# Routing stage of a mixture-of-experts block re-ordered: three tiles gathered within the last tile's logits

## Chip, cores and metric

The kernel runs on one core of one Trainium2 chip. The metric is the device time of one execution in microseconds (us); lower is better. TensorE is PE (its weight loads PEld), VectorE is DVE, ScalarE is ACT, GpSimd is POOL, and SyncE is SP, which here only issues transfers.

## What is computed

One decoder block for 512 tokens of width 1024, in float32: a token mixer (retention heads and gated DeltaNet heads, one input and one output projection), then a mixture of 16 experts in 4 groups of 4. Only the second half matters here:

```python
h = h + gate_m * mixer(xm)                       # ends in the output projection
xf = rms_norm(h) * (1 + scale_f) + shift_f
group = top_1(softmax(xf @ w_group + b_group))   # one of 4 groups
experts = top_2(softmax((xf @ w_router)[group] + b_router))
for each token and each of its two experts e:
    y = (silu(xf @ w_gate[e]) * (xf @ w_up[e])) @ w_down[e]
    out += combine_weight * y
out = rms_norm(h + gate_f * out)
```

## The kernel before

Tokens are handled in four tiles of 128 rows, t = 0 to 3; L is 3, the last. The order of the instructions on each engine is the order in which the code emits them; a framework adds the waits. Every engine works through its own list strictly in order.

**Output projection and routing (lines 1140 to 1376).** For each tile PE makes the output projection in four column blocks q (tile `py`). `stats` makes the new residual `hb` and the scaled rows `xf` on DVE, half a tile at a time, and sums squares on ACT. `scales` turns them into 1/rms (`rs`) with 13 tiny DVE instructions. `turn` transposes half of xf on PE (`xrt`), ACT copies it out (`xrT`), and PE multiplies it with the router's weights (`lg`, `logits`). `xf_rows` scales xf by rs on ACT, adds the row `Brow` and writes the rows to DRAM (`xfd`). `routes` picks group and experts on DVE and leaves a 0/1 mask `M` (token by expert); it runs once for tiles 0 to 2 and once for tile 3. Products of M with triangular and all-one matrices on PE (`pos`) give each token's place in its expert's list. `places` copies them to `posa` and makes the selection matrices `sel01` for experts 0 and 1. `slots` computes addresses, and POOL scatters the token numbers to a list in DRAM, `il`, with two small indirect transfers for each tile. `pick` gathers the rows of experts 0 and 1 by matmuls of xf with sel01 into four PSUM banks `pse` (`xe` in the trace), accumulated over the four tiles.

**Weight parts.** Every weight block of 1 MB is loaded into a raw buffer and split into a high part `hi` (ACT cast, line 293) and a low part `lo` (DVE subtraction, line 294), each in two halves of 128x1024; a product needs three passes of PE. A block is called (expert, j): j = 0 to 3 for gate and up, 4 and 5 for down. `split_next` splits the next one in the order (0,0) to (0,3), (1,0) to (1,3), (0,4), (0,5), (2,0) to (2,3), (1,4), (1,5) and so on. There are six hi/lo pairs and up to eight raw buffers. SP issues the loads in the same order, each one when its raw buffer is free.

**Experts.** For each expert e PE runs `gate_up` (48 matmuls `gu`); after each block j, `after` releases the block's parts and calls split_next for j < 3. DVE multiplies silu(gate) by up (`hh`), PE transposes hh (`xe<-sq,hh`), and `down` (`py`) of expert e runs inside the step of expert e+1. Experts 0 and 1 take their rows from pse (`x_first`: `th`, `tl` for expert 0, `x` for expert 1). From expert 2 on the rows are gathered from xfd by an indirect transfer (`x_load`, tile X) with token numbers `toks`. These come from the list il: POOL loads it (`ilr`), DVE casts it (`ilf`), PE transposes it (`il`) and DVE makes rows and toks (`slot_rows`, called after block (0,0)). `more_blocks` (DVE, called after block (1,0)) plans extra blocks for experts with over 128 tokens; they are worked off inside expert 5's step.

Of the kernel before, what the change touches and what calls it, by code (L numbers as in the profile page):

```python
# [114 lines left out]
def body(ctx, tc, x, c, mod_w, mod_b, norm_mix_w, w_in, gdn_conv_w, gdn_a_log, gdn_dt_bias, gdn_norm_w, w_out,  # L115
# [171 lines left out]
    def split(key, ks=(0, 2048), n=256, n0=256, eng=None):  # L287

        if key not in parts:
            parts[key] = (hi_free.pop(0), lo_free.pop(0))  # L290
        r = loaded[key]
        hi, lo, rw = (flat(t, n)[:, ks[0] // n:ks[1] // n, :n0] for t in (*parts[key], r))
        act.copy(out=hi, in_=rw)  # L293
        (eng or dve).tensor_tensor(out=lo, in0=rw, in1=hi.bitcast(F32), op=ALU.subtract)  # L294
        if ks[1] == 2048:
            free_raw(key)
# [648 lines left out]
    def xT_half(src, half, evac):  # L945

        pt = pst("xrt")
# [238 lines left out]

    def xf_rows(t):
        act.activation(out=xf[t], in_=xf[t], func=AF.Copy, scale=rs[:, t:t + 1])
        pool.tensor_tensor(out=xf[t], in0=xf[t], in1=Brow, op=ALU.add)
        pool.dma_start(out=xfd[t * P:(t + 1) * P], in_=xf[t])  # L1190
# [65 lines left out]
    def places(t0, n):  # L1256

        T = slice(t0, t0 + n)
        dve.tensor_copy(out=posa[:, T], in_=ppos[:, t0 * NE:(t0 + n) * NE].rearrange("p (t e) -> p t e", e=NE))
        for t in range(t0, t0 + n):  # L1260
            for e in range(2):
                dve.tensor_scalar(out=sel01[:, t, e], in0=iota, scalar1=posa[:, t, e:e + 1], scalar2=M[:, t, e:e + 1],
                                  op0=ALU.is_equal, op1=ALU.mult)
# [33 lines left out]
    def turn(t, half, first_):  # L1297

        if first_:
            xts[t] = xT_half(xf[t], half, act.copy)  # L1300
        else:
            logits(pl[:, t * 20:(t + 1) * 20], xts[t], half, True)

    for t in range(NT):
        py = [pst("py") for _ in range(2)]
        for q in range(4):
            w2 = two(("o", q), 256)
            for k in range(KB):
                for i, (a, w) in enumerate(PASSES):
                    pe.matmul(py[q // 2][:, (q % 2) * 256:(q % 2 + 1) * 256], lhsT=mhl[t][a][:, k], rhs=w2[w][:, k],  # L1310
                              start=(k == 0 and i == 0), stop=(k == KB - 1 and i == 2))
                if k == 3 and t and q < 2:
                    turn(t - 1, q, False)
                if k == 3 and q == 2 and t == L:
                    split_next(1, None, pool)
# [9 lines left out]
            if q == 0 and t:  # L1325
                turn(t - 1, 1, True)
            if q == 1:
                if t == L:
                    split_next(1, None, pool)
# [5 lines left out]
                if t:  # L1335
                    xf_rows(t - 1)
            if q == 3:
# [6 lines left out]
    turn(L, 0, False)  # L1344
    turn(L, 1, True)
# [5 lines left out]
    turn(L, 1, False)  # L1351
    places(0, L)
    slots(0, L)
    xf_rows(L)
    pse = [pst("xe") for _ in range(4)]

    def pick(t0, n):

        for t in range(t0, t0 + n):
            for k in range(KB):  # L1360
                pe.matmul(pse[k // 2][:, (k % 2) * 256:(k % 2 + 1) * 256], lhsT=xf[t][:, k * P:(k + 1) * P],
                          rhs=sel01[:, t].rearrange("p e q -> p (e q)"), start=(t == 0 and k % 2 == 0),
                          stop=(t == NT - 1), skip_group_check=True)

    pick(0, L)
    w3 = routes(L, 1)
    for o, l in ((ppos[:, L * NE:NT * NE], stri), (pcn, ones)):
        pe.matmul(o, lhsT=l, rhs=M[:, L], start=False, stop=True, skip_group_check=True)
    places(L, 1)
    cnt = cp.tile([P, NE], F32, name="cnt")  # L1370
    dve.tensor_copy(out=cnt, in_=pcn)
    pick(L, 1)
    slots(L, 1)
    split_next()
# [7 lines left out]
    pool.dma_start(out=ilr, in_=il.rearrange("(r q) o -> r (q o)", q=P))  # L1382
# [267 lines left out]
    for e in range(NE):  # L1650
# [3 lines left out]
        def after(j, e=e):  # L1654
# [143 lines left out]
```

## Time and profile before

| | |
|---|---|
| device time, median of 3 runs | 1088.85 us (1085.78 to 1088.94) |
| the profiled execution | 1089.13 us, its span 1087.3 us |
| PE busy | 963.2 us, 89% of the span |
| DVE busy | 736.0 us, 68% |
| ACT busy | 518.0 us, 48% |
| POOL busy | 295.7 us, 27% |
| DMA | 217.91 MB, mean 200 GB/s |

The span runs from the first to the last instruction of the core; the device time has 1.83 us around it. Busy times of the engines overlap, so they don't add up to the span. All times below count from the start of the span. A line such as `655.32 12.44 PE L1361 MATMUL xe<-sel,xf ... x48 [3.18 <-DVE sel L1262]` reads: 48 instructions of line 1361 began at 655.32 us and took 12.44 us together; PE sat idle 3.18 us before them, until DVE had written sel. The trace counts a float32 matmul twice.

### The profile page before, as it was taken

To read this page: it belongs to the slowest core of one execution; us is meant where nothing else is said; L and a number is where in the kernel's file an instruction comes from. 1 tells how busy PE (TensorE), PEld (TensorE's weight loads), DVE (VectorE), ACT (ScalarE), POOL (GpSimd) and SP (SyncE) were. 2 spreads that over 40 slices of the span, in tenths; PEclk is the share of its full clock that TensorE was granted. 3 is DMA by queue.
4 is the path that set the end of the run, shared out by engine and by line. 5 is a ranking of instruction groups with operands and counts; after the bars stand their busy time and mean duration, and the time that the engine had idled before them with its cause. 6 is when DMAs were issued, how large, how long until landed. Compare 5 with 4: busy or idle time off the path is not lost. (4 is left out here: it accounts for less than half of the span.)

```text
span 1087.3 us, 14839 instructions
## 1 busy us (share of the span) xinstructions
PE 963.2 (89%) x5672; PEld 835.7 (77%) x5672; DVE 736.0 (68%) x1167; ACT 518.0 (48%) x750; POOL 295.7 (27%) x281
## 2 busy tenths in 40 slices
PE   4899989989889999999999977599967899999972
PEld 2579957768799999999989975478846688888851
DVE  3478246767886652566448594699766789898966
ACT  4453134433342331362233333478655778888823
POOL 2018733553447645000000154111100111111103
PEclk8999998989989989999999988799988999999987
DMA  9857742232345532232157245789784799999941
GB/s 297 268 177 249 222 138 83 83 113 82 128 136 145 165 117 79 69 107 79 40 161 252 98 154 75 283 322 388 245 307 171 287 389 384 376 383 365 358 164 78
DMA packets 139538, 217.91 MB, mean 200 GB/s; under 512 B 14942, under 2 KB 72830, under 8 KB 138692
## 3 DMA queue, kind: packets, MB, share of 16 engines
q1 hardware_dynamic: 124640, 182.45, 48.9%
q0 software_dynamic: 11296, 30.66, 9.1%
q10 hardware_dynamic: 3524, 3.78, 1.0%
q8 instruction: 47, 0.77, 0.3%
q14 instruction: 31, 0.25, 0.1%
HBM read 204.98 MB, written 21.16 MB: 208 GB/s over the span
## 5 line engine op out<-in xcount | busy, mean ns | idle before, releaser
L294 DVE TENSOR_TENSOR lo<-raw,hi 128x1024 fp32r<-128x1024 f32 (+1 forms) x194 | 242.0, 1287 | 57.9 <-ACT hi L293 57.8
L293 ACT CAST hi<-raw 128x1024 fp32r<-128x1024 f32 (+1 forms) x198 | 197.4, 1043 | 28.1 <-PE gu L1492 21.6
L1064 PE MATMUL pm<-lo,xh 128*128 128x256 f32 x640 | 186.5, 291 | 11.5 <-DVE ty L650 7.1
L1064 PE MATMUL pm<-hi,xh 128*128 128x256 f32 x640 | 186.5, 291 | 0.0
L1064 PE MATMUL pm<-hi,xl 128*128 128x256 f32 x640 | 185.9, 290 | 0.0
L1064 PEld LDWEIGHTS pm<-lo,xh 128*128 128x128 f32 x640 | 125.8, 196 | 12.4 <-issue 7.2
L1064 PEld LDWEIGHTS pm<-hi,xh 128*128 128x128 f32 x640 | 125.9, 197 | 0.5
L1064 PEld LDWEIGHTS pm<-hi,xl 128*128 128x128 f32 x640 | 125.8, 197 | 0.3
L1492 PE MATMUL gu<-lo,xth 128*128 128x512 f32 x256 | 103.7, 405 | 10.7 <-DVE lo L1559 9.2
L1492 PE MATMUL gu<-hi,xtl 128*128 128x512 f32 x256 | 103.1, 403 | 2.0 <-DVE xtl L1460 2.0
L1492 PE MATMUL gu<-hi,xth 128*128 128x512 f32 x256 | 103.1, 403 | 0.0
L393 POOL TENSOR_TENSOR rawm<-rawm 128x512 f32<-128x512 f32 (+2 forms) x96 | 100.3, 1044 | 7.7
L493 POOL DMA_DIRECT2D rawm<-in_mod_w_dram x32 | 29.7, 927 | 213.8 <-PE modp L510 202.3
L1064 PE MATMUL pm<-xl,hi 128*128 128x512 f32 x168 | 70.1, 417 | 2.0 <-ACT hi L293 1.6
L1064 PE MATMUL pm<-xh,lo 128*128 128x512 f32 x168 | 71.1, 423 | 0.5 <-DVE lo L294 0.5
L1064 PE MATMUL pm<-xh,hi 128*128 128x512 f32 x168 | 70.9, 422 | 0.0
L1492 PEld LDWEIGHTS gu<-lo,xth 128*128 128x128 f32 x256 | 49.4, 193 | 23.4 <-DVE lo L1559 9.6
L1008 ACT ACTIVATE sg<-pm 128x512 f32<-128x512 f32 x32 | 18.9, 597 | 95.9 <-PE pm L1064 81.1
L1514 PE MATMUL py<-lo,th 128*128 128x512 f32 x144 | 61.8, 429 | 1.4 <-ACT th L1505 1.4
L391 POOL TENSOR_TENSOR rawm<-rawm,cs 128x1024 f32<-128x1024 f32 x32 | 61.4, 1918 | 0.6
L1451 POOL DMA_INDIRECT X<-xfd,toks x14 | 20.3, 1448 | 148.8 <-PE xe L1472 128.8
L1492 PEld LDWEIGHTS gu<-hi,xtl 128*128 128x128 f32 x256 | 49.2, 192 | 14.3 <-DVE xtl L1460 2.4
(405 smaller groups left out, 2037.0 us busy)
## 6 DMA issues: line engine op xcount, KB each, us to landing
raw<-in_w_in_dram SPq DMA_DIRECT2D x32, 1024.0 KB
raw<-in_w_up_dram SPq DMA_DIRECT2D x26, 1024.0 KB
raw<-in_w_gate_dram SPq DMA_DIRECT2D x24, 1024.0 KB
raw<-in_w_down_dram SPq DMA_DIRECT2D x20, 1024.0 KB
rawm<-in_mod_w_dram POOLq DMA_DIRECT2D x32, 512.0 KB, 5.2
rawe<-in_w_down_dram SPq DMA_DIRECT2D x9, 1024.0 KB
rawe<-in_w_up_dram SPq DMA_DIRECT2D x8, 1024.0 KB
mod<-in_mod_w_dram SPq DMA_DIRECT2D x7, 1024.0 KB
```

Source lines behind the costliest of these rows:

```text
L293: act.copy(out=hi, in_=rw)
L294: (eng or dve).tensor_tensor(out=lo, in0=rw, in1=hi.bitcast(F32), op=ALU.subtract)
L391: pool.tensor_tensor(out=r, in0=r, in1=cs.unsqueeze(2).to_broadcast([P, KB, n]), op=ALU.mult)
L393: pool.tensor_tensor(out=r[:, :m], in0=r[:, :m], in1=r[:, m:2 * m], op=ALU.add)
L493: pool.dma_start(out=r, in_=mw[:, :, (16 + i) * P:(17 + i) * P])
L1008: act.activation(out=sg, in_=pt, func=AF.Sigmoid)
L1064: pe.matmul(o, lhsT=l, rhs=r, start=st, stop=sp__)
L1451: pool.indirect_dma_start(out=X, out_offset=None, in_=xfd, in_offset=bass.IndirectOffsetOnAxis(ap=at, axis=0), bounds_check=S - 1, oob_is_ ...
L1492: pe.matmul(pt, lhsT=xx[a][k // 4][:, k % 4], rhs=hi_lo[w][:, k % 4], start=(k == 0 and i == 0), stop=(k == KB - 1 and i == 2))
L1514: pe.matmul(pt, lhsT=tt[a][:, k], rhs=hi_lo[w][:, k], start=(k == 0 and i == 0), stop=(k == 3 and i == 2))
```

## The change

In tile 3's step: the low parts of blocks (0,1) and (0,2), which POOL made, are left to DVE and made after the gather; ACT still makes the high parts there. Brow is added by DVE for tiles 2 and 3, and earlier for tiles 0 to 2. The gather (`pick`) of tiles 0 to 2 is interleaved with tile 3's transposes and logits. The list of slots is loaded after the memsets of X, and cast and transposed after block (1,0) instead of (0,0); more_blocks moves to after block (2,0). A split of a block that stood ahead of the experts stands within them.

```diff
-    def split(key, ks=(0, 2048), n=256, n0=256, eng=None):
+    def split(key, ks=(0, 2048), n=256, n0=256, eng=None, what="hl"):
...
-        act.copy(out=hi, in_=rw)
+        if "h" in what:
+            act.copy(out=hi, in_=rw)
+        if "l" not in what:
+            return
         (eng or dve).tensor_tensor(out=lo, in0=rw, in1=hi.bitcast(F32), op=ALU.subtract)
...
+    def xf_scale(t):
+        act.activation(out=xf[t], in_=xf[t], func=AF.Copy, scale=rs[:, t:t + 1])
+
     def xf_rows(t):
-        act.activation(out=xf[t], in_=xf[t], func=AF.Copy, scale=rs[:, t:t + 1])
-        pool.tensor_tensor(out=xf[t], in0=xf[t], in1=Brow, op=ALU.add)
+        (pool if t < L - 1 else dve).tensor_tensor(out=xf[t], in0=xf[t], in1=Brow, op=ALU.add)
         pool.dma_start(out=xfd[t * P:(t + 1) * P], in_=xf[t])
...
+    def split_upper():
+
+        key = order[nsplit[0] + len(held_back)]
+        for h in (0, 1):
+            split(key, (h * 1024, h * 1024 + 1024), 512, 512, what="h")
+        held_back.append(key)
+
     def split_next(n=1, half=None, eng=None):
         for _ in range(n):
+            if held_back:
+                key = held_back.pop(0)
+                for h in (0, 1):
+                    split(key, (h * 1024, h * 1024 + 1024), 512, 512, what="l")
+                nsplit[0] += 1
+                continue
...
             if q == 0 and t:
                 turn(t - 1, 1, True)
+                xf_scale(t - 1)
+                xf_rows(t - 1)
             if q == 1:
                 if t == L:
-                    split_next(1, None, pool)
+                    split_upper()
                     w012 = routes(0, L)
...
-                if t:
-                    xf_rows(t - 1)
-            if q == 3:
+            if q == 3 and t < L:
                 turn(t, 0, True)
...
-    turn(L, 0, False)
-    turn(L, 1, True)
     pe.matmul(ppos[:, :L * NE], lhsT=stri, rhs=M[:, :L].rearrange("p t e -> p (t e)"), start=True, stop=False,
...
+    turn(L, 0, True)
+    places(0, L)
+    selections(0)
+    stats(L, 1, py[1])
+    selections(1)
+    selections(2)
+    slots(0, L)
+    scales(L, 1)
+    pse = [pst("xe") for _ in range(4)]
...
+    pick(0)
+    turn(L, 0, False)
+    turn(L, 1, True)
+    pick(1, range(4))
     turn(L, 1, False)
-    places(0, L)
-    slots(0, L)
-    xf_rows(L)
...
-    pick(0, L)
+    xf_scale(L)
     w3 = routes(L, 1)
+    pick(1, range(4, KB))
+    pick(2)
     for o, l in ((ppos[:, L * NE:NT * NE], stri), (pcn, ones)):
         pe.matmul(o, lhsT=l, rhs=M[:, L], start=False, stop=True, skip_group_check=True)
+    xf_rows(L)
     places(L, 1)
+    selections(L)
...
-    pick(L, 1)
+    pick(L)
     slots(L, 1)
-    split_next()
...
-    pool.dma_start(out=ilr, in_=il.rearrange("(r q) o -> r (q o)", q=P))
...
     def slot_rows():
 
+        dve.tensor_copy(out=ilf, in_=ilr)
         pt = ps_m.tile([P, 512], F32, tag="m", name="il")
...
     for t in (X, X2):
         pool.memset(t, 0.0)
+    pool.dma_start(out=ilr, in_=il.rearrange("(r q) o -> r (q o)", q=P))
...
-            if e == 0 and j == 0:
+            if e == 1 and j == 0:
                 slot_rows()
                 x_load(toks[:, 8:9], X)
-            if e == 1 and j == 0:
+            if e == 2 and j == 0:
                 more_blocks()
...
         if e == 0:
+            split_next()
             xx1 = x_first(1)
-            split_next(2)
+            split_next(4)
```

On PE, from tile 3's transposes (`xrt`) and logits (`lg`) to the last gather (`xe`), the list of before reads as follows (`sel_5062` is sel01, `pos` the list products):

```order
L950 MATMUL xrt<-sq_94,xf_5055 128x128 x4
L957 MATMUL lg<-wr,xrT 128x20 x4
L950 MATMUL xrt<-sq_94,xf_5055 128x128 x4
L1346 MATMUL pos<-M,sq_94 128x48
L1348 MATMUL pos<-Mc,ones 128x48
L1350 MATMUL pos<-Mc,ones 128x16
L957 MATMUL lg<-wr,xrT 128x20 x4
L1361 MATMUL xe<-sel_5062,xf_5054 128x256 x16
L1361 MATMUL xe<-sel_5062,xf_5055 128x256 x8
L1368 MATMUL pos<-M,sq_94 128x16
L1368 MATMUL pos<-M,ones 128x16
L1361 MATMUL xe<-sel_5062,xf_5055 128x256 x8
```

In the change the three list products of tiles 0 to 2 come first, and the last of them heads this piece of PE's list:

```order
L1369 MATMUL pos<-Mc,ones 128x16
L953 MATMUL xrt<-sq_94,xf_5055 128x128 x4
L1383 MATMUL xe<-sel_5062,xf_5054 128x256 x8
L960 MATMUL lg<-wr,xrT 128x20 x4
L953 MATMUL xrt<-sq_94,xf_5055 128x128 x4
L1383 MATMUL xe<-sel_5062,xf_5054 128x256 x4
L960 MATMUL lg<-wr,xrT 128x20 x4
L1383 MATMUL xe<-sel_5062,xf_5054 128x256 x4
L1383 MATMUL xe<-sel_5062,xf_5055 128x256 x8
L1397 MATMUL pos<-M,sq_94 128x16
L1397 MATMUL pos<-M,ones 128x16
L1383 MATMUL xe<-sel_5062,xf_5055 128x256 x8
```

The gather of tiles 0 to 2 has moved from behind the logits to between and behind them; the number of matmuls is the same.

On DVE, from the end of the gather to expert 0's `hh`, before (raw_4776 holds block (1,0), raw_88 (1,1), raw_5037 (1,2), raw_89 (1,3), raw_4775 at the end (0,4)):

```order
L1460 TENSOR_TENSOR tl<-xe,th 128x256 x4
L1593 CAST ilf<-ilr 64x128
L1460 TENSOR_TENSOR x_5912<-xe,x_5912 128x256 x4
L294 TENSOR_TENSOR lo_5036<-raw_4776,hi_5035 128x1024 x2
L294 TENSOR_TENSOR lo_5901<-raw_88,hi_5900 128x1024 x2
L294 TENSOR_TENSOR lo_5460<-raw_5037,hi_5459 128x1024 x2
L1396 CAST rows<-il 128x64
L1397 COPY rowsf<-il 128x64
L1401 TENSOR_SCALAR toks<-rows 128x64
L294 TENSOR_TENSOR lo_93<-raw_89,hi_92 128x1024 x2
L294 TENSOR_TENSOR lo_91<-raw_4775,hi_90 128x1024 x2
L1498 TENSOR_TENSOR hh<-hh,gu_5885 128x512
```

The same place on DVE with the change (blocks (0,1), then (0,2), (0,3), (1,0), (1,1), (1,2), (1,3), (0,4)):

```order
L1490 TENSOR_TENSOR tl<-xe,th 128x256 x4
L297 TENSOR_TENSOR lo_93<-raw_5037,hi_92 128x1024 x2
L1490 TENSOR_TENSOR x_5903<-xe,x_5903 128x256 x4
L297 TENSOR_TENSOR lo_91<-raw_89,hi_90 128x1024 x2
L297 TENSOR_TENSOR lo_5034<-raw_4775,hi_5033 128x1024 x2
L297 TENSOR_TENSOR lo_5036<-raw_4776,hi_5035 128x1024 x2
L297 TENSOR_TENSOR lo_5893<-raw_88,hi_5892 128x1024 x2
L297 TENSOR_TENSOR lo_5463<-rawe_5894,hi_5462 128x1024 x2
L297 TENSOR_TENSOR lo_93<-rawe_5895,hi_92 128x1024 x2
L297 TENSOR_TENSOR lo_91<-raw_5037,hi_90 128x1024 x2
L1528 TENSOR_TENSOR hh<-hh,gu_5873 128x512
```

Three blocks more stand between the gather and hh, and the cast of the list is gone. It stands in expert 1's part of DVE's list now, behind the subtraction of block (2,0), which takes the pair that block (1,0) frees:

```order
L1528 TENSOR_TENSOR hh<-hh,gu_5873 128x512
L297 TENSOR_TENSOR lo_5034<-raw_89,hi_5033 128x1024 x2
L1536 TENSOR_TENSOR tl<-xe,th 128x512
L297 TENSOR_TENSOR lo_5036<-raw_4775,hi_5035 128x1024 x2
L1423 CAST ilf<-ilr 64x128
L1426 CAST rows<-il 128x64
L1427 COPY rowsf<-il 128x64
L1431 TENSOR_SCALAR toks<-rows 128x64
```

Here lo_5036<-raw_4775 is block (2,0). On PE the transpose `il` has moved with the cast, from behind block (0,0) to behind block (1,0).

## Rows read from the trace of the kernel before

**Rows 1.** Stretches: us, busy (count) by engine, granted clock, DMA share, GB/s

```profile
640.30:655.30 15.00, 6.30 (x31) 5.94 (x31) 14.27 (x26) 6.18 (x10) 7.59 (x5) 0.67 0.41 153
676.40:688.10 11.70, 0.00 (x0) 0.00 (x0) 0.24 (x2) 4.44 (x5) 2.43 (x3) 0.63 0.86 264
688.10:693.30 5.20, 5.17 (x13) 4.03 (x14) 5.20 (x8) 1.04 (x1) 0.00 (x0) 0.51 0.12 17
693.30:701.70 8.40, 5.94 (x26) 4.44 (x24) 8.40 (x12) 6.92 (x7) 1.30 (x1) 1.00 0.98 345
721.80:740.00 18.20, 18.20 (x86) 14.71 (x86) 17.66 (x19) 14.90 (x18) 3.25 (x2) 1.00 1.03 379
```

**Rows 2.** Timeline of PE, 628 to 689 us

```profile
628.08 0.96 PE L957 MATMUL lg<-wr,xrT 128*128 128x20 f32 x8
...
640.06 0.28 PE L1310 MATMUL py<-hi,ml 128*128 128x256 f32 x1
643.12 0.63 PE L950 MATMUL xrt<-sq,xf 128*128 128x128 f32 x4 [2.78 <-DVE xf L1176]
646.51 1.90 PE L957 MATMUL lg<-wr,xrT 128*128 128x20 f32 x8 [2.76 <-ACT xrT L952]
...
655.32 12.44 PE L1361 MATMUL xe<-sel,xf 128*128 128x256 f32 x48 [3.18 <-DVE sel L1262]
667.60 0.29 PE L1368 MATMUL pos<-M,sq 128*128 128x16 f32 x2
...
669.11 3.69 PE L1361 MATMUL xe<-sel,xf 128*128 128x256 f32 x16 [1.00 <-DVE sel L1262]
...
688.13 0.37 PE L1395 MATMUL il<-sq,ilf 64*128 64x64 f32 x1 [11.76 <-DVE ilf L1593]
```

**Rows 3.** Timeline of DVE, 635 to 702 us

```profile
635.41 2.08 DVE L1211 TENSOR_TENSOR w<-lg,m 128x60 f32<-128x60 f32 x1
...
647.12 4.99 DVE L1184 TENSOR_TENSOR rs<-ssq 128x1 f32<-128x1 f32 x1
...
673.29 1.42 DVE L1460 TENSOR_TENSOR tl<-xe,th 128x256 fp32r<-128x256 f32 x4 [1.24 <-ACT th L1459]
...
688.00 1.40 DVE L1460 TENSOR_TENSOR x<-xe,x 128x256 fp32r<-128x256 f32 x4
689.33 6.88 DVE L294 TENSOR_TENSOR lo<-raw,hi 128x1024 fp32r<-128x1024 f32 x6
...
701.04 0.67 DVE L1498 TENSOR_TENSOR hh<-hh,gu 128x512 f32<-128x512 f32 x1
```

**Rows 4.** Line 1361 in 657 to 659 and in 661 to 667 us: durations in ns

```profile
L1361 PE MATMUL xe<-sel,xf x6: 477/634/634, 656.7 to 658.9; 128*128 128x256 f32 x6
L1361 PE MATMUL xe<-sel,xf x30: 379/379/379, 660.7 to 667.0; 128*128 128x256 f32 x30
```

**Rows 5.** Timelines of ACT and DVE: the split of block (2,0)

```profile
703.87 1.05 ACT L293 CAST hi<-rawe 128x1024 fp32r<-128x1024 f32 x1 [0.82 <-PE gu L1492]
705.28 1.05 ACT L293 CAST hi<-rawe 128x1024 fp32r<-128x1024 f32 x1 [0.35 <-PE gu L1492]
...
706.36 1.23 DVE L294 TENSOR_TENSOR lo<-rawe,hi 128x1024 fp32r<-128x1024 f32 x1 [0.18 <-ACT hi L293]
```

**Rows 6.** Timelines of DVE and PE: the last of more_blocks, expert 1's transposes

```profile
713.19 0.17 DVE L1401 TENSOR_SCALAR ovtok<-ovrow 128x7 int32<-128x7 int32 x1
...
718.56 0.66 PE L1503 MATMUL xe<-sq,hh 128*128 128x128 f32 x4 [1.21 <-DVE hh L1498]
```

**Rows 7.** Tile X in 640 to 730 us: its gathers

```profile
DMA to landing us min/median/max: 7.0/7.0/7.0
```

**Rows 8.** Stretch with the scatters' transfers, columns as in rows 1

```profile
672.00:678.00 6.00, 3.87 (x16) 2.48 (x14) 1.47 (x5) 5.12 (x12) 0.97 (x1) 1.00 0.73 38
```

**Rows 9.** Timeline of POOL, 683 to 686 us

```profile
683.16 0.57 POOL L1382 DMA_DIRECT2D ilr<-il  x1 [10.10 <-DMA il<-tok,slots]
683.73 1.87 POOL L1597 MEMSET X<- 128x1024 f32 x2
```

More of the change, by code (lines that the diff above doesn't have):

```diff
@@ L943, in open_out, with xT_half @@
         pool.tensor_copy(out=tok, in_=crt[:, 20:28])
-    def xT_half(src, half, evac):
-        pt = pst("xrt")
+    def xT_half(src, half, evac, m=False):
+        pt = ps_m.tile([P, 512], F32, tag="m", name="xrt") if m else pst("xrt")
         for k in range(4):
@@ L1259, in places, with selections @@
         dve.tensor_copy(out=posa[:, T], in_=ppos[:, t0 * NE:(t0 + n) * NE].rearrange("p (t e) -> p t e", e=NE))
[L1260 to L1263, printed above, removed]
+    def selections(t):
+        for e in range(2):
+            dve.tensor_scalar(out=sel01[:, t, e], in0=iota, scalar1=posa[:, t, e:e + 1], scalar2=M[:, t, e:e + 1],
+                              op0=ALU.is_equal, op1=ALU.mult)
     def slots(t0, n):
@@ L1280, in body @@
     nsplit = [0]
+    held_back = []
+    def split_upper():
[3 more added lines that the diff above has]
+        held_back.append(key)
     def split_next(n=1, half=None, eng=None):
         for _ in range(n):
+            if held_back:
[4 more added lines that the diff above has]
+                continue
             if nsplit[0] < len(order) and (hi_free or half) and order[nsplit[0]] in loaded:
@@ L1299, in turn @@
         if first_:
-            xts[t] = xT_half(xf[t], half, act.copy)
+            xts[t] = xT_half(xf[t], half, act.copy, t == L)
         else:
@@ L1326, in body @@
                 turn(t - 1, 1, True)
+                xf_scale(t - 1)
+                xf_rows(t - 1)
             if q == 1:
                 if t == L:
-                    split_next(1, None, pool)
+                    split_upper()
                     w012 = routes(0, L)
@@ L1350, in body, with pick @@
     pe.matmul(pcn, lhsT=ones, rhs=Mc[:, L], start=False, stop=False, skip_group_check=True)
-    turn(L, 1, False)
-    places(0, L)
-    slots(0, L)
-    xf_rows(L)
[L1355 to L1363, printed above, removed]
-    pick(0, L)
+    turn(L, 0, True)
[7 more added lines that the diff above has]
+    pse = [pst("xe") for _ in range(4)]
+    def pick(t, ks=range(KB)):
+        for k in ks:
+            pe.matmul(pse[k // 2][:, (k % 2) * 256:(k % 2 + 1) * 256], lhsT=xf[t][:, k * P:(k + 1) * P],
+                      rhs=sel01[:, t].rearrange("p e q -> p (e q)"), start=(t == 0 and k % 2 == 0),
+                      stop=(t == NT - 1), skip_group_check=True)
+    pick(0)
+    turn(L, 0, False)
+    turn(L, 1, True)
+    pick(1, range(4))
+    turn(L, 1, False)
+    xf_scale(L)
     w3 = routes(L, 1)
+    pick(1, range(4, KB))
+    pick(2)
     for o, l in ((ppos[:, L * NE:NT * NE], stri), (pcn, ones)):
         pe.matmul(o, lhsT=l, rhs=M[:, L], start=False, stop=True, skip_group_check=True)
+    xf_rows(L)
     places(L, 1)
+    selections(L)
     cnt = cp.tile([P, NE], F32, name="cnt")
     dve.tensor_copy(out=cnt, in_=pcn)
-    pick(L, 1)
+    pick(L)
     slots(L, 1)
-    split_next()
     for i in range(len(scatters)):
@@ L1592, in body @@
     ilf = cp.tile([NE * 4, P], F32, tag="vec", name="ilf")
-    dve.tensor_copy(out=ilf, in_=ilr)
-    more_parts((13, 14))
     X, X2 = (em.tile([P, D], F32, name=n) for n in ("X", "X2"))
@@ L1597, in body @@
         pool.memset(t, 0.0)
+    pool.dma_start(out=ilr, in_=il.rearrange("(r q) o -> r (q o)", q=P))
+    more_parts((13, 14))
     rl_free += [em.tile([P, 2048], F32, name=f"rawe{i}") for i in range(RE - 1)]
```

## The prediction

> **What bounds the kernel now.** I began with the page: PE is busy for most of the span, so I looked for stretches in which it is not. The table of stretches shows two about the change [rows 1]: from 640.3 to 655.3 us PE works 6.3 of 15 us at a granted clock of 0.67, and from 676.4 to 688.1 it does nothing. From 721.8 to 740 it has no gap (18.20 of 18.20), and that is the pace of one expert. So time can be won only between the end of tile 3's projection and the first experts. PE's timeline [rows 2] names what PE waited for: the projection ends at 640.34 (640.06 + 0.28); then come gaps of 2.78 (xf of tile 3), 2.76 (its copy xrT) and 3.18 us (sel), the gather to 672.80 with one gap, and 11.76 us for ilf, the cast of the slots' list. DVE's timeline [rows 3] shows why sel was late: one addition on a 128x1 column (rs, line 1184) took 4.99 us, until POOL's subtractions beside it had ended, and a routing step took 2.08 us beside another of them. After 688.00 DVE works without a gap until hh of expert 0 at 701.71 (701.04 + 0.67), for which PE waits 2.5 us at the end of a stretch in which it was busy 5.94 of 8.40 [rows 1]. So three things end last one after another: routing, the list, and DVE's subtractions ahead of hh.
>
> **Term 1, to the end of the gather.** In the new order PE follows the projection with the list products, copies of xf, and the gather of tile 0, with little to wait for. From 640.34 I add:
> - products, posa and the first two selections: 1.8 us. The later pair of products with its selections takes 1.5 from 667.60 to 669.11 [rows 2]; here are three products instead of two.
> - the gather of three tiles, 48 instructions. They start 0.217 us apart at full clock (29 steps from 660.7 to 667.0) and 0.44 apart at half (5 steps from 656.7 to 658.9) [rows 4]. The gaps that lowered the clock are gone in the new order, so I take 0.217: 10.4 us.
> - two halves of logits at 0.96 (row 628.08, full clock) and one transposed half at 0.63, which in this order lie between gathers: 2.5 us. The first transposes run while DVE makes the selections.
> - the products and selections of tile 3: 1.5 us; its gather: 3.69 us (669.11) [rows 2].
>
> The sum is 640.34 + 1.8 + 10.4 + 2.5 + 1.5 + 3.7 = 660.2, against 672.8: **12.6 us** gained. DVE's part beside it (tile 3's second stats, four selections, addresses, rs, then routing of tile 3) is covered: PE's 3.5 us of gather for tile 0, half of tile 1 and the logits lie over the first, 5.2 us of the rest over routing. Where that cover failed, each us would count. Brow's two additions on DVE cost what two halves of a block cost, 1.2 us each: tile 2's stands ahead of the routing of tiles 0 to 2, which loses its wait beside POOL (2.08 us for a short step [rows 3]) and isn't asked for before 640.3; tile 3's lies under the gather of tile 2. The six scatters are queued on POOL earlier; nobody on PE waits for them.
>
> **Term 2, from the gather to hh of expert 0.** Before, it took from 672.80 to 701.71, 28.9 us, of which DVE idled 13 for the list [rows 2, 3]. Now DVE has no wait there but more work: tl ends 1.9 us after the gather (673.29 + 1.42 against 672.80); block (0,1) is 2.3 (6.88 for three blocks); x 1.35 (688.00 to 689.33); seven more blocks 16.05; hh 0.67 [rows 3]. That is 22.3 us: **6.6 us** gained, and hh ends at 682.5 instead of 701.7. PE's gate_up of expert 0 (48 products at 5.94/26 = 0.23 us each [rows 1], 11 us and a wait of about one more for the low parts) ends some 12.5 us after the gather, so PE idles about 10 us for hh. Two unknowns, each with both ends:
> - The memsets of X (1.87 us on POOL [rows 9]) now fall beside the subtractions. If they block DVE as POOL's subtractions did, they cost up to 1.9. The nearest row of a blocked DVE is that of rs [rows 3], but that was beside a subtraction, which reads two tiles; a memset reads nothing. I take 0. The Trainium skill, page "SBUF — State Buffer", section "Who interferes with whom", says that a DVE instruction with two inputs in SBUF contends with a GpSimd instruction that reads SBUF, not with one that only writes it. By that rule the memsets cost nothing and the sum stays; by a plain lock of both engines it would be 1.9 less. No row here shows a memset of this size beside a busy DVE.
> - Blocks (1,2) and (1,3), loaded early before, now go into buffers that are free only after the last gather, and later loads queue behind them on SP. DVE asks for (1,2) 14.8 us after the gather, for (0,4) after 19.4, and ACT needs 2 us before. Beside the scatters' small transfers the DMA moved only 38 GB/s for 6 us [rows 8], and afterwards 264 [rows 1]; three blocks would so be in after some 15 us, in time. I take 0; the other end is with the rivals.
>
> **Term 3, experts 1 and 2.** Four prices come in:
> - After 10 us of idling PE starts expert 1 at half clock. Before, after 11.76 us, PE took 5.2 us for 12 products (clock 0.51) that at 0.23 are 2.8 [rows 1]: 2.3 us; and this now comes in expert 1, where there was full clock.
> - The list. Its transpose stands behind block (1,0) on PE, its cast on DVE behind the subtraction of (2,0), which needs the pair that (1,0) frees. In the trace that split took from 705.28 (released by PE) to 707.59 [rows 5]; with a cast of 0.25 PE waits 2.6 us, and works 0.35 on the transpose. That is 2.9 us. The list itself is there by then: POOL waited 10.10 us for the scatters to land [rows 9], and cast and load came 4.7 us after that, some 15 us after the last scatter; in the new order this is about 675, 12 us ahead of its use.
> - X of expert 2 is gathered after toks and lands 7.0 us after its issue [rows 7], issued about a us after toks. That is when gate_up of expert 1 ends: 0 to 1.2 us, I take 0.6.
> - more_blocks took DVE from 707.6 to 713.3 [rows 5, 6] and made PE wait 1.21 us for hh of expert 1 (718.56). In expert 2's step, with x's low parts beside it, I count a wait of 1.6: 0.4 more.
>
> Term 3 is 2.3 + 2.9 + 0.6 + 0.4 = **6.2 us** lost. From expert 3 on the lists are as before, and everything later moves with it.
>
> **Sum.** 12.6 + 6.6 - 6.2 = 13.0. The profiled execution took 1089.1 us, within 0.3 of the median; 1089.1 - 13.0 = **1076.1 us**. With the list and the clock of term 3 free of cost it would be 1071; with memsets (1.9), loads (2.6, below), a later X (0.6) and half of the slow clock below in expert 1 (3.5) it would be 1084.7.
>
> **Rivals.**
> - *The clock stays at half* (ends slower). If the gather and expert 1 run at 1.2 GHz throughout, 64 gather instructions cost 0.223 more each (14.3), logits, transposes and products about 2 more, and 36 products of expert 1 0.2 each (7). 13.0 - 23.3 is a loss of 10: 1099. It decides once a little over half of that work is slow. For it: after gaps of 2.78 and 2.76 us the gather began at half clock [rows 2, 4], and 640 to 655 had 0.67 [rows 1]. Against it: the remaining gaps of the new order are under 1 us, and a gap of 2.5 us before 701.7 left the clock at 1.00 [rows 1]. The Trainium skill, page "TensorE: Matmul & The Clock Gate", section "Part 4: PE-mode transpose", says that transposes don't count as busy time for the clock as other matmuls do; by that rule the new interleaving would lean to this rival. The full clock of the logits' row among transposes speaks neither way, since projection products surround it.
> - *Loads late.* If the buffers of (1,2) and (1,3) are filled only when the last scatters have landed, 10 us after their issue [rows 9], about 671.5, block (0,4) lands some 20 us after the gather, and hh waits 2.6 us: 1078.7, and up to 1084 if the DMA stays slow for 6 us more [rows 8].
> - *A new wait eats more of it.* The list's wait grows if expert 1's first block is still at half clock and DVE is behind; 2.9 becomes up to 6, and the clock costs another 3: 1082.
> - *Hidden anyway.* DMA is at 1.03 and 379 GB/s while PE is full [rows 1]. If loads set the pace of experts 1 to 5, the gain is given back there: 1088. Against it: loads start when buffers become free, which is earlier too, and PE shows no gap at that pace.
>
> **How the numbers follow.** Forecast 0.62 (its own range 1071 to 1081), loads late 0.13, new wait 0.10, hidden 0.07, slow clock 0.08. Runs of this kernel differ by about 0.3%, 3.3 us, which is what a measurement can tell from no change. Faster by more: the first three, 0.85; within: 0.07; slower: 0.08. The range of 1069 to 1085 leaves out the last two and little of the others.
>
> **What the changed profile would show.** Right: the last gather ends near 660, at clock 1.0; rs and routing steps have no duration of 2 us or more; DVE is busy without a gap from there to hh near 682.5; PE has one gap of about 10 us before expert 0's transposes and one of about 2.6 before `il`, with clock near 0.5 behind the first. Wrong: gather instructions 0.44 us apart; DVE waiting for `hi` of (1,2) to (0,4) with ACT waiting for DMA; a gap before `il` above 5 us; PE waiting in experts 3 to 5.

## Result and profile after

The changed kernel took 1077.43 us (median of 4 runs, 1075.6 to 1078.26) against 1088.89 for the kernel before, a ratio of 0.9898 with a 95% interval of 0.9875 to 0.9921. Run again later (`changed_again`, below) it took 1075.43 against 1085.49: 0.9915, 0.9885 to 0.9944. The forecast was 1076.1. The profiled execution took 1078.26 us, its span is 1076.5.

PE's timeline of the changed kernel, from the last product of the projection to the transposes of X in expert 3's step (739.45):

```profile
636.31 0.28 PE L1331 MATMUL py<-hi,ml 128*128 128x256 f32 x1
...
638.20 3.69 PE L1383 MATMUL xe<-sel,xf 128*128 128x256 f32 x16 [0.55 <-DVE sel L1268]
...
645.55 5.43 PE L1383 MATMUL xe<-sel,xf 128*128 128x256 f32 x24
...
652.23 3.72 PE L1383 MATMUL xe<-sel,xf 128*128 128x256 f32 x16 [0.90 <-DVE sel L1268]
...
680.82 1.11 PE L1533 MATMUL xe<-sq,hh 128*128 128x128 f32 x4 [10.98 <-DVE hh L1528]
...
688.98 0.34 PE L1425 MATMUL il<-sq,ilf 64*128 64x64 f32 x1 [2.52 <-DVE ilf L1423]
...
699.23 1.03 PE L1502 MATMUL xe<-sq,X 128*128 128x128 f32 x8
...
717.38 1.03 PE L1502 MATMUL xe<-sq,X 128*128 128x128 f32 x8
...
723.51 1.11 PE L1533 MATMUL xe<-sq,hh 128*128 128x128 f32 x4 [2.30 <-DVE hh L1528]
...
739.45 1.03 PE L1502 MATMUL xe<-sq,X 128*128 128x128 f32 x8
```

The gaps ahead of the gather are down from 2.78, 2.76 and 3.18 us [rows 2] to 0.55 and 0.90. The last gather ends at 655.95. One wait of 11 us has moved from the list to hh, and the list's transpose has 2.52 us of its own. The same X transposes in the kernel before, PE's timeline:

```profile
713.51 1.03 PE L1472 MATMUL xe<-sq,X 128*128 128x128 f32 x8
...
733.05 1.04 PE L1472 MATMUL xe<-sq,X 128*128 128x128 f32 x8
...
751.19 1.04 PE L1472 MATMUL xe<-sq,X 128*128 128x128 f32 x8
```

Stretches of the changed kernel, columns as in [rows 1]:

```profile
636.60:655.95 19.35, 17.90 (x98) 15.59 (x97) 11.95 (x52) 4.87 (x8) 9.10 (x16) 1.00 0.49 52
669.00:680.80 11.80, 0.84 (x4) 0.36 (x2) 9.28 (x9) 8.57 (x9) 0.00 (x0) 0.63 1.04 386
680.80:688.98 8.18, 5.63 (x16) 4.30 (x16) 5.54 (x6) 3.81 (x5) 0.00 (x0) 0.70 1.04 386
688.98:699.20 10.22, 10.22 (x37) 8.08 (x38) 5.36 (x7) 5.64 (x6) 1.08 (x1) 0.83 1.03 368
699.20:717.40 18.20, 18.20 (x86) 14.78 (x85) 16.17 (x30) 14.91 (x18) 2.70 (x2) 1.00 1.02 372
717.40:739.40 22.00, 19.70 (x85) 15.82 (x84) 21.70 (x27) 15.05 (x18) 2.66 (x2) 0.92 0.89 307
```

The granted clock (third column from the right) is 1.00 through the whole gather and falls three times afterwards, not once. DVE's timeline, from rs to hh of expert 0:

```profile
641.94 0.15 DVE L1187 TENSOR_TENSOR rs<-ssq 128x1 f32<-128x1 f32 x1
...
656.51 1.42 DVE L1490 TENSOR_TENSOR tl<-xe,th 128x256 fp32r<-128x256 f32 x4 [3.52 <-issue]
657.85 2.35 DVE L297 TENSOR_TENSOR lo<-raw,hi 128x1024 fp32r<-128x1024 f32 x2
...
661.45 9.16 DVE L297 TENSOR_TENSOR lo<-raw,hi 128x1024 fp32r<-128x1024 f32 x8
670.52 2.35 DVE L297 TENSOR_TENSOR lo<-rawe,hi 128x1024 fp32r<-128x1024 f32 x2
674.50 2.36 DVE L297 TENSOR_TENSOR lo<-rawe,hi 128x1024 fp32r<-128x1024 f32 x2 [1.63 <-ACT hi L294]
677.23 2.36 DVE L297 TENSOR_TENSOR lo<-raw,hi 128x1024 fp32r<-128x1024 f32 x2 [0.36 <-ACT hi L294]
680.08 0.69 DVE L1528 TENSOR_TENSOR hh<-hh,gu 128x512 f32<-128x512 f32 x1 [0.49 <-ACT hh L1527]
```

rs takes 0.15 us instead of 4.99 [rows 3]. But DVE isn't busy throughout: it waits for ACT's high parts of blocks (1,3) and (0,4), and for silu: 1.63 + 0.36 + 0.49 = 2.5 us.

From such rows each kernel has five lengths, in us. A: from the projection's end to the gather's end. B: from there to the end of hh of expert 0. C: to X's transposes in expert 1's step. D and E: from there to those in expert 2's and in expert 3's step. A step with no wait takes 18.15 to 18.2; a D of 19.16 or 19.18 holds a wait of 0.8 us for hh of expert 1.

| kernel | projection ends | A | B | C | D | E | A to E |
|---|---|---|---|---|---|---|---|
| before | 640.34 | 32.46 | 28.91 | 11.80 | 19.54 | 18.14 | 110.9 |
| changed | 636.59 | 19.36 | 24.82 | 18.46 | 18.15 | 22.07 | 102.9 |
| changed_again | 634.25 | 19.36 | 24.28 | 18.52 | 18.15 | 22.09 | 102.4 |
| old_list_late | 638.09 | 32.51 | 15.72 | 17.84 | 18.14 | 22.22 | 106.4 |
| list_early | 637.91 | 19.36 | 29.40 | 11.79 | 18.18 | 20.66 | 99.4 |
| pool_parts | 639.25 | 26.89 | 18.97 | 16.37 | 18.17 | 22.22 | 102.6 |
| late_gather | 635.81 | 24.44 | 22.07 | 18.93 | 18.18 | 22.24 | 105.9 |
| list_first | 637.58 | 19.36 | 23.07 | 14.00 | 18.25 | 20.65 | 95.3 |
| more_late | 638.54 | 19.36 | 25.22 | 18.09 | 18.18 | 18.18 | 99.0 |
| warm | 638.39 | 19.36 | 23.24 | 16.31 | 18.18 | 22.11 | 99.2 |
| hh_first | 635.62 | 19.36 | 15.25 | 16.04 | 18.18 | 22.99 | 91.8 |
| both | 636.16 | 19.37 | 15.25 | 14.13 | 19.18 | 18.18 | 86.1 |
| hh_first_spread | 640.56 | 19.36 | 15.26 | 14.53 | 19.16 | 18.15 | 86.5 |

Between the two profiles the change gained 13.1 in A and 4.1 in B and lost 9.2 in C to E: 8.0 us. Another 3.75 us lie ahead of the stage, in work that the change doesn't touch, and 0.9 were lost behind it: 8.0 + 3.75 - 0.9 = 10.8, the difference of the spans. They are there before the projection begins (its first product starts at 583.03 us before and at 579.38 with the change), and the projection's end varies from 634.25 to 640.56 over these executions, so I put them down to chance (last section). That isn't settled: the interval of the first comparison, 8.6 to 13.6 us, lies just above the stage's 8.0, and that of the second, 6 to 12.5, holds it.

### The profile page after: what moved, and what is told of

The parts are those of the page before. It is cut to its first block, busy times and chain, and to the rows that moved or that the text cites. A ratio compares the mean times of both kernels' runs of the same rounds, so it can differ in the third digit from the quotient of the medians.

```text
span 1076.5 us, 14837 instructions
## 1 busy us (share of the span) xinstructions
PE 959.5 (89%) x5672; PEld 831.2 (77%) x5672; DVE 731.7 (68%) x1173; ACT 518.3 (48%) x750; POOL 279.9 (26%) x275
## 5 line engine op out<-in xcount | busy, mean ns | idle before, releaser
L297 DVE TENSOR_TENSOR lo<-raw,hi 128x1024 fp32r<-128x1024 f32 (+1 forms) x200 | 245.5, 1268 | 63.8 <-ACT hi L294 63.6
L294 ACT CAST hi<-raw 128x1024 fp32r<-128x1024 f32 (+1 forms) x200 | 199.2, 1043 | 21.1 <-PE gu L1522 18.2
L1067 PEld LDWEIGHTS pm<-lo,xh 128*128 128x128 f32 x640 | 125.2, 196 | 12.5 <-issue 7.2
```

Source lines behind the costliest of these rows:

```text
L1067: pe.matmul(o, lhsT=l, rhs=r, start=st, stop=sp__)
```

## Experiments

Times of runs move by some us for that reason, so each kernel is given by its ratio to the kernel before on the same chip, and read by its lengths A to E.

**The parts of the change, each undone or made alone.**

`list_early`:

```diff
-            if e == 1 and j == 0:
+            if e == 0 and j == 0:
                 slot_rows()
```

> The changed kernel with one condition back: the slots' list is taken up behind the first block of expert 0, as before the change. Theory: the list's move is worth little by itself, because PE now waits 11 us for hh of expert 0 anyway. With it early, PE stops at the list's transpose behind block (0,0) until about 672, gate_up of expert 0 ends near 685 and hh of expert 0 some 5 us later than 680.8; expert 1 then runs without the 2.5 us list wait and at full clock (3.8 us back). Sum within 3 us of the changed kernel's 1077.4. Rival: the whole list wait of before (11.8 us) comes back and nothing is won in expert 1: 1086 to 1089.

1075.61 us against 1084.62 (0.9904; 0.9874 to 0.9933). PE waited 13.46 us for the list's cast and then 0.98 for hh, which ended 4.6 us later than in the changed kernel (B 29.40). C fell to 11.79, the value of before: no list wait, full clock. A to E is 3.5 us shorter than with the list late (3.0 against `changed_again`). The theory held, but 1.4 of that stand in E, which the edit doesn't touch: the wait of 2.29 us there wasn't followed by a fall of the clock. So the move of the list costs 1.6 to 3.5 us in the new order, too little to show between the runs' times.

`old_list_late` (the kernel before with only the list, its cast and load, and more_blocks moved):

```diff
...
-            if e == 0 and j == 0:
+            if e == 1 and j == 0:
                 slot_rows()
...
-            if e == 1 and j == 0:
+            if e == 2 and j == 0:
                 more_blocks()
```

> The kernel before with only the list part of the change: list taken up in expert 1, overflow bookkeeping in expert 2, cast and load of the list moved. Theory: hh of expert 0 is ready about 19 us behind the gather instead of 28.9 (two blocks are done by GpSimd already), 9 to 10 us won; the list wait, the half clock behind the idle and the bookkeeping in expert 2 take 7 to 9 of it back: 1085.5 to 1088.5. Rival: the list is what the change lives on, 1079 to 1082.

1080.66 against 1084.62 (0.9962; 0.9937 to 0.9986). B fell by 13.2, more than the 9 to 10 expected; C and E gave back 10.1, D won 1.4. The time lies in the rival's range, but only because the kernel before ran 4 us faster here than the 1088.85 that both ranges start from; as a gain, 4.0 us in time and 4.4 in A to E, it lies between the two theories. So the same move gains 4.4 us in the old order and loses 1.6 to 3.5 in the new: there it took away the last thing that PE waited for, here DVE's parts end last either way.

`pool_parts`:

```diff
                 if k == 3 and q == 2 and t == L:
-                    split_upper()
+                    split_next(1, None, pool)
...
                 if t == L:
-                    split_upper()
+                    split_next(1, None, pool)
...
-            split_next()
             xx1 = x_first(1)
-            split_next(4)
+            split_next(3)
```

> The changed kernel with the two subtractions of blocks (0,1) and (0,2) put back on GpSimd during tile 3's projection; everything else stays. Theory: DVE is blocked beside them again (single short steps of 2 to 5 us), routing and selections come later, PE gets gaps of 2 to 3 us before the gather, which ends 4 to 6 us later; the 4.7 us of subtractions that DVE is spared ahead of hh of expert 0 give at most 2 back, since the loads of (1,2) to (0,4) are late there. 1079 to 1082. Rival: DVE's work ahead of hh is what counts, so that 4.7 us come off and the kernel is at 1074 or below.

1077.15 against 1084.62 (0.9931; 0.9895 to 0.9967). DVE's timeline in this kernel, the steps beside POOL's subtractions:

```profile
633.51 5.02 DVE L1216 TENSOR_TENSOR w<-lg,m 128x60 f32<-128x60 f32 x1
...
645.40 2.60 DVE L1176 TENSOR_TENSOR hb<-hb,xf 128x512 f32<-128x512 f32 x1
648.04 2.73 DVE L1179 TENSOR_TENSOR xf<-hb,Srow 128x512 f32<-128x512 f32 x1
```

And POOL's:

```profile
633.70 4.74 POOL L297 TENSOR_TENSOR lo<-raw,hi 128x1024 fp32r<-128x1024 f32 x2
...
645.10 5.12 POOL L297 TENSOR_TENSOR lo<-raw,hi 128x1024 fp32r<-128x1024 f32 x2 [6.66 <-ACT hi L294]
```

A step of 0.22 us took 5.02, additions of 0.7 took 2.6 and 2.7; A grew by 7.5. But DVE was spared two blocks: B fell by 5.9, and PE's shorter wait for hh gave 2.1 in C. A to E is the same as with the change (102.6 against 102.9). I had capped that return at 2: neither theory held. POOL's subtractions cost the gather what they save ahead of hh.

`late_gather`, the order of code in tile 3's step as before:

```diff
-            if q == 3 and t < L:
+            if q == 3:
                 turn(t, 0, True)
...
-    turn(L, 0, True)
+    turn(L, 0, False)
+    turn(L, 1, True)
+    turn(L, 1, False)
     places(0, L)
     selections(0)
-    stats(L, 1, py[1])
     selections(1)
     selections(2)
     slots(0, L)
-    scales(L, 1)
+    xf_scale(L)
...
     pick(0)
-    turn(L, 0, False)
-    turn(L, 1, True)
-    pick(1, range(4))
-    turn(L, 1, False)
-    xf_scale(L)
+    pick(1)
+    pick(2)
     w3 = routes(L, 1)
-    pick(1, range(4, KB))
-    pick(2)
```

> The changed kernel with the old order of the routing stage (logits of tile 3 in full, then selections, addresses, the gather of three tiles, routing of tile 3), without GpSimd's subtractions. Theory: the gaps before the gather come back (about 2.8 us each for xf and its copy, and one for sel), the clock falls, the last gather ends 6 to 9 us later after the projection's end than the 19.4 us of the changed kernel, hh of expert 0 follows by as much: 1082 to 1086. Rival: hh of expert 0 waits for the loads anyway, so that a later gather costs at most 2 us: 1078 to 1079.5.

1080.5 against 1084.62 (0.9956; 0.9933 to 0.998). The gather ended 5.1 us later. The gaps on PE were small (1.21 and 0.67 us for xrT, none for sel), but the gather behind them began at a low clock, 0.57:

```profile
642.26:648.00 5.74, 5.74 (x17) 4.65 (x18) 5.19 (x25) 0.28 (x1) 3.24 (x6) 0.57 0.01 0
```

So the gather of three tiles took 13.02 us instead of the 10.4 of full clock, half of the 5.1. Of these 5.1 us, 2.75 came back in B, where DVE had no wait left because the loads had more time; A to E is 3.0 longer. Between the two theories: half of what the interleaving wins is lost to late loads.

**The loads and the clock.**

`no_scatter`:

```diff
     def slots(t0, n):
...
-            for i in range(2):
-                pool.memset(spacer, 0.0)
-                scatters.append(pool.indirect_dma_start(
...
+            pass
```

> The changed kernel without the eight scatters of slots (so the list stays at its initial value and the rows of X aren't fetched); read only up to hh of expert 0. Theory: the loads of (1,2) and (1,3), issued at the gather's end and landed 12.9 and 17 us later, wait behind the scatters' small transfers; without them (1,2) lands within 5 us, DVE doesn't wait for ACT there, and hh of expert 0 ends 22.3 us behind the gather instead of 24.8. Rival: they wait for something else (SP's queue, buffers): still 24.5 to 25.

B was 22.07 us; forecast for it, without late loads, 22.3. The changed kernel, ACT's timeline, and two stretches:

```profile
668.97 2.00 ACT L294 CAST hi<-rawe 128x1024 fp32r<-128x1024 f32 x2 [4.88 <-DMA rawe<-in_w_up_dram]
673.43 1.99 ACT L294 CAST hi<-rawe 128x1024 fp32r<-128x1024 f32 x2 [2.47 <-DMA rawe<-in_w_up_dram]
676.15 1.99 ACT L294 CAST hi<-raw 128x1024 fp32r<-128x1024 f32 x2 [0.73 <-DMA raw<-in_w_down_dram]
```

```profile
656.00:661.00 5.00, 4.47 (x19) 3.60 (x20) 4.49 (x9) 4.89 (x11) 1.85 (x2) 1.00 0.76 18
661.00:666.00 5.00, 4.15 (x16) 2.57 (x15) 5.00 (x7) 3.09 (x4) 0.00 (x0) 1.00 0.89 105
```

The same of the kernel without scatters:

```profile
664.80 3.93 ACT L294 CAST hi<-rawe 128x1024 fp32r<-128x1024 f32 x4
669.29 1.99 ACT L294 CAST hi<-raw 128x1024 fp32r<-128x1024 f32 x2 [0.55 <-DVE lo L297]
```

```profile
656.00:661.00 5.00, 4.42 (x19) 3.23 (x18) 3.62 (x7) 4.02 (x10) 2.34 (x3) 1.00 0.56 180
661.00:666.00 5.00, 4.70 (x20) 3.48 (x19) 5.00 (x9) 5.00 (x7) 0.00 (x0) 1.00 1.03 374
```

With the scatters the DMA engines are 76% busy and move 18 GB/s; without them 180, then 374, and ACT waits for no load. B is 23.07 to 25.22 in the five executions with the changed kernel's work up to hh (`changed`, `changed_again`, `list_first`, `more_late`, `warm`), so the scatters' small transfers cost 1.0 to 3.2 us there, as far as the one execution without them tells. The Trainium skill, page "DMA: Bandwidth & Descriptors", section "Issuing engines are not separate DMA queues", says that transfers started by different engines run on the same DMA engines and interleave there; these stretches agree (18 against 180 GB/s).

`warm`:

```diff
+        if e == 0:
+            for _ in range(44):
+                pe.matmul(banks['ht'][:, :P], lhsT=ident, rhs=ones, start=True, stop=True)
         tts[e] = h_prep(hh)
```

> The changed kernel with 44 products of two constants (128x128, results unused) issued on PE behind gate_up of expert 0, where PE waits 11 us for hh. Theory: it was that wait that let the clock fall, and the half clock costs 3 to 4 us in expert 1; with PE busy the products of expert 1 run at full clock, hh of expert 0 to X of expert 2 goes from 18.5 to 15 to 16.5 (the list wait stays or grows a little, since DVE's cast comes when it came). Rival: the half clock lay over time that PE would have spent waiting for the list anyway: 17.5 to 18.5, nothing won.

1074.13 against 1085.49 (0.9907; 0.9871 to 0.9942). PE's timeline (each product counts twice, so 88):

```profile
670.22 9.98 PE L1742 MATMUL xe<-ones,sq 128*128 128x128 f32 x88
681.04 0.66 PE L1533 MATMUL xe<-sq,hh 128*128 128x128 f32 x4 [0.83 <-DVE hh L1528]
681.45 0.48 PE L1522 MATMUL gu<-lo,x 128*128 128x512 f32 x1
...
687.03 0.27 PE L1425 MATMUL il<-sq,ilf 64*128 64x64 f32 x1 [2.52 <-DVE ilf L1423]
687.24 0.80 PE L1522 MATMUL gu<-lo,x 128*128 128x512 f32 x1
```

The transposes took 0.66 instead of 1.11 and C 16.31 instead of 18.46: the half clock behind the wait for hh costs 2.1 us. But the list wait of 2.52 that follows drops the clock a second time (a product of 0.48 takes 0.80). So in the changed kernel two falls lie in C.

`list_first`:

```diff
+            if e == 1 and j == 0:
+                slot_rows()
+                x_load(toks[:, 8:9], X)
             if j < (3 if e != EC else 0):
                 split_next()
-            if e == 1 and j == 0:
-                slot_rows()
-                x_load(toks[:, 8:9], X)
```

> The changed kernel with the list taken up ahead of the subtraction of block (2,0) in expert 1, not behind it. Times from the end of the projection to the transposes of X in expert 3 (before 110.9, changed 102.9). Theory: the 2.5 us that PE waits for ilf are only DVE's order, so they go, and the half clock behind expert 0's wait ends no later: 100 to 100.5 on that stretch, the whole 2 to 3 us less than the changed kernel. Rival: the half clock lasts a fixed amount of work, and PE without the wait meets the next block's subtraction instead: 102 to 103, no change.

1073.51 against 1084.99 (0.9896; 0.9864 to 0.9927). The list wait is gone and C fell by 4.5: 2.5 of wait and 2 of the second fall of the clock, as these stretches show:

```profile
680.00:685.20 5.20, 5.13 (x17) 4.02 (x17) 3.10 (x5) 2.81 (x4) 0.00 (x0) 0.63 1.05 387
685.20:694.00 8.80, 8.80 (x38) 6.79 (x37) 7.58 (x9) 6.71 (x7) 1.29 (x1) 1.00 1.04 385
```

A to E is 7.5 shorter, three times the theory's 2.5: 1.75 of it in B and 1.4 in E, where the same wait of 2.29 us for hh wasn't followed by a fall of the clock; these two are chance of this execution, as far as the edit tells.

**What bounds it now.**

`more_late`:

```diff
-            if e == 2 and j == 0:
-                more_blocks()
...
         if e == 2:
+            more_blocks()
             ws_gen += [w012, w3]
```

> The changed kernel with the overflow bookkeeping put behind hh of expert 2 on DVE instead of behind its first block. Theory: hh of expert 2 no longer waits (2.3 us) and the clock doesn't fall there; X to X in that step goes from 22.1 to about 18.2, the stretch from the projection's end from 102.9 to 99, and nothing comes back later since DVE's lead over PE is several blocks. 3.5 to 4 us less. Rival: DVE has no lead, and 5.8 us of bookkeeping turn up as a wait in expert 3: no change or slower.

1074.26 against 1084.99 (0.9891; 0.985 to 0.9932). E is 18.18, but the next step took 22.8 (its X at 760.37, after 737.57). PE's timeline there:

```profile
744.28 0.66 PE L1533 MATMUL xe<-sq,hh 128*128 128x128 f32 x4 [2.87 <-DVE hh L1528]
```

The rival held: the wait moved to expert 3. Counted to that step the kernel is at 121.8, the changed one at 121.0.

`hh_first`:

```diff
-            if j < (3 if e != EC else 0):
+            if e and j < (3 if e != EC else 0):
                 split_next()
...
-            if e == 1 and j == 0:
-                slot_rows()
-                x_load(toks[:, 8:9], X)
...
+        elif e == 0:
+            slot_rows()
+            x_load(toks[:, 8:9], X)
+            split_next(4)
         elif not last:
             split_next()
```

> The changed kernel with hh of expert 0 and the list put ahead of four of the subtractions that stood before it on DVE (blocks (1,2), (1,3), (0,4), (0,5)). Theory: expert 0's hh waits for DVE's order alone: hh ends some 15.5 us behind the gather instead of 24.8, PE's wait shrinks from 11 to about 2.5 us, the clock stays up (3.8 us) and the list wait goes (2.5): X of expert 2 some 14 us earlier, of which the bookkeeping in expert 2 and a smaller lead of DVE take up to 5 back: 9 to 14 us less than the changed kernel. Rival: the loads set the pace (DMA at 1.03 from 664 to 716), so PE gets waits for parts in experts 1 to 3 and the gain is 5 us or less.

1064.14 against 1084.99 (0.9822; 0.9783 to 0.9862), better than both kernels. B is 15.25, as the theory had it, and A to E 11.0 shorter than the changed kernel's. Three of the four blocks had stood ahead of hh, (1,2), (1,3) and (0,4); (0,5) had stood behind it. PE's timeline, its two remaining waits:

```profile
671.53 0.36 PE L1425 MATMUL il<-sq,ilf 64*128 64x64 f32 x1 [3.93 <-DVE ilf L1423]
671.82 1.12 PE L1533 MATMUL xe<-sq,hh 128*128 128x128 f32 x4
...
711.36 0.66 PE L1533 MATMUL xe<-sq,hh 128*128 128x128 f32 x4 [3.07 <-DVE hh L1528]
```

The transposes at 1.12 show that the clock fell here too, behind 3.93 us. That wait ends with the list: hh was ready at 670.23, and DVE then had to wait for the list's load:

```profile
671.25 0.22 DVE L1423 CAST ilf<-ilr 64x128 f32<-64x128 int32 x1 [1.02 <-DMA ilr<-il]
```

ACT waits up to 0.75 us a block for loads from 674 us on, but PE shows no wait for parts in experts 1 to 3: the DMA pace was not the bound.

`both` is hh_first with the edit of more_late.

> hh_first and more_late together. Theory: the two gains stand in different experts and add up: 12 to 17 us less than the changed kernel. Rival: with hh early DVE has no lead left, so that the bookkeeping behind hh of expert 2 shows up as a wait of 3 to 6 us for expert 3's parts: no better than hh_first alone.

1064.53 against 1084.99 (0.9833; 0.9771 to 0.9896). A to E won 5.7 over hh_first, the next step took 23.3: the rival held again.

`hh_first_spread` is hh_first with a `yield` behind each operation of more_blocks, two of which are emitted behind each block from expert 2 on:

```diff
-            if e == 2 and j == 0:
-                more_blocks()
...
-        if e == 2:
-            ws_gen += [w012, w3]
+        if e == 1:
+            ws_gen += [more_blocks(), w012, w3]
```

> hh_first with the overflow bookkeeping cut into single operations, two behind each block of experts 2 to 4. Theory: the bookkeeping costs a wait (3.1 us at hh of expert 2 in hh_first) only because 5.8 us of it stand in one place; at 1.2 to 2.7 us for each expert it fits in DVE's free time (16.8 of 18.2 us), so the wait and the half clock behind it go: 3 to 4 us less than hh_first's 1064. Rival: DVE has no free time until its lead is rebuilt, so that small waits in experts 2 to 4 add up to as much: 1063 to 1065.

1060.34 against 1085.49 (0.9766; 0.9728 to 0.9803), the lowest median of all; its runs (1057.82 to 1065.42) overlap with those of `hh_first` (1063.73 to 1068.51), so the gain of the spreading is read from the lengths. E is 18.15 and the step behind it 18.3: the bookkeeping is hidden. (The 1.0 more in D is there in `both` as well, where no bookkeeping stands in that step.)

`changed_again` is the changed kernel, unedited.

> The changed kernel again, beside the others. Theory: the stretch from the projection's end to X of expert 3 repeats within 1 us (102.9), while the time at which the projection ends, in code that the change doesn't touch, moves by some us from execution to execution with the clock behind earlier waits; so the kernels' difference on this chip is nearer 8 us than the 10.9 between the two profiles. Rival: the change itself makes the early part 3.7 us shorter, so the projection ends near 636.6 again and the difference is 10.5 or more.

1075.43 against 1085.49. A to E repeats to 0.5 us. The projection ended at 634.25, 2.3 us earlier than in the first profile of the same kernel and 6.3 earlier than in `hh_first_spread`. Its difference in time, 10.1 us with a ratio between 0.9885 and 0.9944, is nearer to the rival's number; with that interval (6 to 12.5 us) it doesn't decide.

## Why the prediction was right, step by step

- **Term 1 held.** Predicted 19.9 us from the projection's end to the gather's end, measured 19.36: 13.1 gained, not 12.6. What hides DVE's part held too, and the clock stayed at 1.00, so the rival of the slow clock fell. The Trainium skill's rule on transposes (page "TensorE: Matmul & The Clock Gate", "Part 4: PE-mode transpose") leaned to that rival; with one transposed half between the gathers and one ahead of them the trace shows no fall here. In `late_gather`, with both halves and all logits ahead of the gather, the clock was down behind them; whether the transposes or the two gaps did that, no run tells. Undoing either cause costs A 5.1 (`late_gather`) or 7.5 us (`pool_parts`).
- **Term 2 was mis-sized by 2.5 us**: B 24.8 instead of 22.3 (24.3 in `changed_again`). The price of DVE's own work was right (22.07 in `no_scatter`). The step that failed is "three blocks would so be in after some 15 us, in time. I take 0": (1,2) came 13 us after the gather, (1,3) 17.5, (0,4) 20.2, which is the rival of late loads with its price of 2.6. Its own rates already give 17 us, not 15 (6 us at 38 GB/s, the rest of three blocks at 264), just before ACT needs (0,4); and the slow time lasted some 10 us, at 18 and then 105 GB/s, not 6. So DVE had gaps, where the prediction had named a DVE without any as a sign of being right.
- **The memsets at 0 held, but not where they were expected.** POOL's timeline of the changed kernel shows them beside DVE's tl (656.51, above), which took 1.42 us as before [rows 3], and over by the time the subtractions start (657.85). tl reads one of its two inputs, xe, from PSUM. The rule of the Trainium skill (page "SBUF — State Buffer", section "Who interferes with whom") is about a DVE instruction with two inputs in SBUF; no run here shows such a one beside a memset of this size. POOL's line:

```profile
656.07 1.85 POOL L1625 MEMSET X<- 128x1024 f32 x2 [0.54 <-issue]
```

- **Term 3 was mis-sized by 3.0 us**: 9.2 lost instead of 6.2. The list wait was right (2.52 against 2.6), and the transpose too (0.3). X of expert 2 made no wait (0.6 expected). The clock was counted once, at 2.3; it fell behind the wait for hh, behind that for the list, and behind that for hh of expert 2. In C: 18.46 - 11.80 - 2.52 - 0.3 = 3.84 for two falls, of which `warm` measures the first at 2.1. In E: 22.07 - 18.15 = 3.9, of which 2.30 are the wait, and 1.6 the third fall; the 1.4 that the wait cost in expert 1 before went away. So moving more_blocks cost 2.5, not 0.4; in `list_early` and `list_first`, where that third fall is missing (E 20.7), it cost 1.1.
- **The sum was nearer than its terms.** The stage gained 8.0, not 13.0. Between the two profiles another 3.75 us came from ahead of the stage, and 0.9 went behind it. The forecast of faster is right, and the mechanism is right in every step but the loads and the number of falls. That the time came within 1.4 us of the median is partly luck: the gain in the stage was forecast 5 us too large, and the medians' 11.5 us hold 3.5 that the stage doesn't explain and the prediction didn't speak of.
- **Hidden anyway** fell: waits for loads held DVE ahead of hh of expert 0 only, and the steps where nothing else held PE took 18.15 us (D, and the two behind E).

## What to carry to other kernels

A wait that is removed uncovers the next: after the change PE waited 11 us for hh, of which 2.5 were late loads and most of the rest the order of the queues. `hh_first`, which takes three blocks out from ahead of that one short step and has the list right behind it, gained more in the stage (11.0 us) than the whole change (8.0). Price every expected wait of PE for itself and, with a chance of its own, for the half clock that may follow (from nothing to some 2 us here), and ask where small transfers are in flight when large loads are due. Work that is cut into single operations fits into an engine's free time; the same 5.8 us moved as a block only move the wait.

## What was not expected of the hardware

- Waits of 2.3 to 2.5 us in the middle of busy work lowered the clock (behind the list at 688.98, behind hh at 723.51, transposes at 1.11); yet behind 2.53 us in the kernel before it stayed up (transposes at 0.66, below; C 11.80), and waits of 3.07 and 2.87 (`hh_first`, `more_late`) left the four transposes right behind them at 0.66, the fall coming after. Eight kernels of the table have the wait of 2.3 us for hh in E; six show a fall behind it (E about 22.1), `list_early` and `list_first` none (20.7). The length of a wait alone doesn't tell whether or when the clock falls. PE's timeline of the kernel before:

```profile
701.77 0.66 PE L1503 MATMUL xe<-sq,hh 128*128 128x128 f32 x4 [2.53 <-DVE hh L1498]
```

- The same instructions behind the same wait (2.22 us for sg near 391 us) run at different clocks in different executions. The stretch 385 to 400 us, columns as above, of the kernel before, of the changed kernel, and of the changed kernel again:

```profile
385.00:400.00 15.00, 12.78 (x81) 12.58 (x80) 10.96 (x19) 4.88 (x6) 7.99 (x8) 0.76 0.38 123
```

```profile
385.00:400.00 15.00, 12.78 (x97) 12.58 (x95) 11.05 (x20) 4.88 (x6) 8.01 (x6) 0.89 0.37 112
```

```profile
385.00:400.00 15.00, 12.78 (x109) 12.58 (x109) 12.40 (x18) 4.88 (x6) 8.89 (x8) 1.00 0.33 107
```

PE gets 81, 97 or 109 instructions done in the same 15 us. The projection's end moves by up to 6.3 us over 13 profiles. That the clock behind such waits is what moves it is read from them, and not tried by an experiment of its own.
